# All products pass by pass, and new byte places for the operands of TensorE

## The chip, the cores and the metric

The kernel runs on one core of a Trainium2 chip. The metric is the device time of one execution in microseconds (us). Matrix products run on TensorE: the page calls its matmuls PE and its weight loads PEld. VectorE is DVE, ScalarE ACT, GpSimd POOL, SyncE SP. A matmul has a stationary operand, the weights (128 x 128, loaded before it), and a moving operand, here 128 partitions by 256 or 512 columns of 4 bytes, that streams past the weights.

## The reference

A trunk of two layers over 256 tokens with a model width of 1024, in float32. `swiglu` stands four times: before and after each layer's mixer.

```
x = x + 0.5 * swiglu(rmsnorm(x, norm_w[l, 0]), w_gate, w_up, w_down)     # d_ff = 2816
x = x + mixer(rmsnorm(x, norm_w[l, 1]))   # l = 0: Mamba-2 (SSD), l = 1: windowed attention over shared k, v
x = x + 0.5 * swiglu(rmsnorm(x, norm_w[l, 2]), ...)
swiglu(h) = (silu(h @ w_gate) * (h @ w_up)) @ w_down
```

k and v are computed once from the residual stream after layer 0. A final RMSNorm ends it.

## The kernel before

**Three products for one.** To keep float32 precision, each operand is split into a high part (rounded to the type float32r) and a low part (what the rounding left). A product is high x high + high x low + low x high: three matmuls per 128 x 128 block. Weights come from memory in chunks of 2 x 512 KB (`raw`); ACT writes the high part `hi` (L144), DVE the low part `lo` (L155), each a tile of 128 x 1024 in one pool of six buffers. A tile of weights is called a unit; `ORDER` lists the units, and `tick`, called after each, issues the rounding of later ones. SP issues the loads.

**First products.** The normed input lies in eight tiles `xs0` to `xs7`, each 128 x 512: the high part `xh` in the left 256 columns, the low part `xl` in the right 256. Units g and u (gate and up) go through `wide` (L354): a matmul of 512 columns does hi x xh and hi x xl at once, and one of 256 does lo x xh. Units dt, B, C, x, z (Mamba mixer) and qA, qB (attention) go through `unit` (L339), all with 256 columns. kA, kB and v use tiles of their own, `xkh` and `xkl`.

**Second products.** Units d (down), so (mixer out) and ao (attention out) go through `rows` (L372): for each of eight output blocks j, three matmuls of 256 columns with the moving operands `hh` and `hl` (also named `yh`, `yl`, `oh`, `ol`).

**Stages.** f0, the Mamba mixer, f1, f2, attention, f3. f0 to f3 are the four `swiglu`; each has 22 steps f of one g, one u and (from f = 4 on) one d unit, 16 + 16 + 24 = 56 matmuls, plus four d units behind. f2 also holds kA and kB (48 matmuls on L349).

**The order of the passes before.** The order on every engine is written out by hand. In `wide`, f1 and f2 (`l != i`) from f = 1 on run the eight 512-wide matmuls of `hi` and then the eight 256-wide of `lo` ("pass by pass"); f0 and f3 alternate, one of `hi`, one of `lo`. In `rows`, f1 and f2 run (hi,hh), (hi,hl), (lo,hh); all others (hi,hh), (lo,hh), (hi,hl). In `unit`, the x units and the very first unit run pass by pass, the others alternate.

**Places.** Tiles lie one behind another in the pools, so a tile's first byte falls at some place within a 512-byte block; a step of 128 columns of weights is 512 bytes, so all blocks of a weight tile, and all eight `xs` tiles, share a place. In the built program before: `hi` and `lo` at 160, `xs` at 480, `hh` and `hl` at 480, `xkh` and `xkl` at 160. The tile `ones`, which the warm-up uses for both operands, is at 128.

Of the kernel before, what the change touches and what calls it, by code (L numbers as in the profile page):

```python
# [9 lines left out]
F32 = mybir.dt.float32  # L10
F32R = mybir.dt.float32r
# [5 lines left out]
P = 128  # L17
T = 256
D = 1024
KT = D // P  # L20
# [13 lines left out]
CH = 2  # L34
RAW = 4
NEG = -1.0e30


def ffn_order(l, i):
# [36 lines left out]
ORDER = order()  # L76
# [33 lines left out]
class Weights:  # L110
# [38 lines left out]
    def low(self, half=None):  # L149
        u = self.cut  # L150
        c, i = divmod(u, CH)
        if not half:
            self.lo = self.parts.tile([P, D], F32R, tag="lo", name=f"lo{u}")
        hi, lo, s = self.ready.get(u, self.hi), self.lo, self.piece(half)
        self.nc.vector.tensor_tensor(lo[:, s], self.chunks[c][:, i, s], hi[:, s].bitcast(F32), ALU.subtract)  # L155
        if half == 0:
            return
        self.ready[u] = (hi, lo)
        self.cut += 1
        if i == CH - 1 or u == NU - 1:  # L160
            del self.chunks[c]
            self.load()
# [53 lines left out]
class Trunk:  # L216
    def __init__(self, ctx, tc, a):
# [2 lines left out]
        self.NPART = 6  # L220
        cp = self.cp = ctx.enter_context(tc.tile_pool(name="const", bufs=1))

        self.op = ctx.enter_context(tc.tile_pool(name="op", bufs=LAG + 2))
        top = ctx.enter_context(tc.tile_pool(name="top", bufs=1, side="right"))
        self.wk = ctx.enter_context(tc.tile_pool(name="work", bufs=2))
        raw = ctx.enter_context(tc.tile_pool(name="raw", bufs=RAW))
        parts = ctx.enter_context(tc.tile_pool(name="parts", bufs=self.NPART))
# [108 lines left out]
        nc.scalar.copy(rs, b[:, 0:256])  # L336
        return rs

    def unit(self, what, out, xh=None, xl=None, before=None):  # L339

        nc = self.nc
        xh = self.xh if xh is None else xh
        xl = self.xl if xl is None else xl
        hi, lo = self.W.next(what)
        passes = [(k, w, x) for k in range(KT) for w, x in ((hi, xh), (hi, xl), (lo, xh))]
        if self.W.pos == 1 or what[0] == "x":
            passes = [(k, w, x) for w, x in ((hi, xh), (lo, xh), (hi, xl)) for k in range(KT)]
        for n, (k, w, x) in enumerate(passes):
            nc.tensor.matmul(out, w[:, k * P : (k + 1) * P], x[k], start=n == 0, stop=n == len(passes) - 1)  # L349
        if before:  # L350
            before()
        self.tick()
# [16 lines left out]
        self.slots.run()  # L369
        self.W.ahead(self.NPART - 2)  # L370

    def rows(self, units, accs, first, last, done=None, high_first=False):  # L372

        nc = self.nc
        for j in range(KT):
            out = accs[j % 4][:, (j // 4) * T : (j // 4) * T + T]
            s = slice(j * P, (j + 1) * P)
            for n, ((hi, lo), hh, hl) in enumerate(units):
                f, e = first and n == 0, last and n == len(units) - 1
                passes = ((hi, hh), (hi, hl), (lo, hh)) if high_first else ((hi, hh), (lo, hh), (hi, hl))  # L380
                for m, (w, x) in enumerate(passes):
                    nc.tensor.matmul(  # L382
                        out, w[:, s], x, start=f and j < 4 and m == 0, stop=e and m == 2, skip_group_check=True
                    )
            if done:
                done(j, out)
# [90 lines left out]
    def ffn(self, l, i, key, nxt):  # L477
        nc, wk = self.nc, self.fw
# [24 lines left out]
        def product(name, f, t):  # L503

            b = self.bank(f"{name}_{key}_{f}")
            if self.W.pos == 0:
                self.slots.at(0, lambda: nc.scalar.copy(t, b[:, 0:T]))
                self.unit((name, l, i, f), b[:, 0:T])
                return

            def add():
                nc.scalar.copy(t, b[:, T:])  # L512
                nc.vector.tensor_tensor(t, b[:, 0:T], t, ALU.add)  # L513

            self.slots.at(0, add)
            self.wide((name, l, i, f), b, by_part=l != i and f > 0)

        for f in range(NF):
            g, u = (wk.tile([P, T], F32, tag=n, bufs=4, name=f"{n}s_{key}_{f}") for n in "gu")
# [14 lines left out]
    def down(self, l, i, f, hs, accs):  # L534
        hi_lo = self.W.next(("d", l, i, f))
        hh, hl = hs.pop(f)
        self.rows([(hi_lo, hh, hl)], accs, f == 0, False, high_first=l != i)
        self.tick()

    def tail(self, units, accs, nxt):  # L540
# [7 lines left out]
    def ssm(self, nxt):  # L548
# [9 lines left out]
        accs = []  # L558
# [264 lines left out]
        for what in seq[:-2]:  # L823
            if what[0] == "so":
                tt = what[1]
                if not accs:
                    accs = self.accs("sa")
                self.rows([(self.W.next(what), yh[tt], yl[tt])], accs, tt == 0, False)
                self.tick()
            else:  # L830
                o = half()
                self.unit(what, o, before=lambda: evac(what, o, E[what] - at[what]))
        self.tail([(w, yh[w[1]], yl[w[1]]) for w in seq[-2:]], accs, nxt)


# [29 lines left out]

    def split_k(self):
        wk = self.kp
        self.xkh = [wk.tile([P, T], F32R, name=f"xkh{k}") for k in range(KT)]
        self.xkl = [wk.tile([P, T], F32R, name=f"xkl{k}") for k in range(KT)]
        for k in range(KT):  # L870
# [34 lines left out]
    def att(self, nxt):  # L905
# [124 lines left out]
        for j in range(4):  # L1030
# [3 lines left out]
                sl.at(0, lambda: vdone(vb))  # L1034
                self.shared_v(1, vb)
            b = self.bank(f"q{j}")
            self.unit(("qA", j), b[:, 0:T])
            Q[j] = [wk.tile([P, T], F32, tag=f"Q{r}", name=f"Q{j}_{r}") for r in range(2)]

            def q_rope(j=j, b=b):  # L1040
# [194 lines left out]
```

## Time and profile before

| | before |
|---|---|
| median of 3 runs | 1048.29 us (1047.95 to 1049.29) |
| profiled execution | 1048.69 us |
| its span, first to last instruction | 1046.9 us |
| PE busy | 1025.2 us (98%), 7290 records |
| PEld busy | 948.2 us (91%) |
| DVE / ACT / POOL busy | 775.1 / 627.7 / 79.4 us |
| DMA | 190.84 MB, mean 182 GB/s |

The 1.8 us between the execution and its span lie before the first and behind the last instruction. Matmuls are pipelined: one that is busy for 278 ns overlaps the next, so the distance between the starts of two, not the duration, tells how fast they go. A timeline row of N matmuls runs from the start of the first to the end of the last; the chain's pieces follow each other without overlap, so a piece of N matmuls divided by N is their spacing. Some fp32 matmuls (warm-up, statistics) have two records each.

### The profile page before, as it was taken

Reading aid. Unit: us, or ns where it says so; the run is one execution under the profiler, and the core shown is the slowest. Engines: PE = TensorE matmul, PEld = TensorE weight load, DVE = VectorE, ACT = ScalarE, POOL = GpSimd, SP = SyncE. Lnnn points to the kernel's source line nnn. Section 1 sums busy time; section 2 is a strip of 40 time slices with the busy share of each in tenths; the row PEclk is TensorE's granted clock in tenths of the full one; section 3 lists DMA queues with packets and bytes.
Section 4 is the critical chain, followed back from the end, with each engine's and each line's share of the span. In section 5 each row is a group of like instructions: output and inputs, shape, how many; then the busy total and the mean of one; then the engine's idle time right before and its main releaser. Section 6 shows DMA issues by size and latency. Waiting matters only on the chain.

```text
span 1046.9 us, 18340 instructions
## 1 busy us (share of the span) xinstructions
PE 1025.2 (98%) x7290; PEld 948.2 (91%) x7290; DVE 775.1 (74%) x1420; ACT 627.7 (60%) x1106; POOL 79.4 (8%) x122
## 2 busy tenths in 40 slices
PE   8999999999999999999999999999999999999996
PEld 7899999999989898999999899999998888999996
DVE  4766666788999977766667796666689777666664
ACT  6555555669877756555555664555565766555554
POOL 3000000210110112000000200000031020000000
PEclk9999999999999999999999999999999999999998
DMA  8555554546545354555455455554554244555521
GB/s 304 195 201 176 186 200 164 194 171 252 217 156 213 131 201 153 197 201 200 169 203 200 157 211 200 177 209 178 202 202 152 92 161 167 196 186 191 187 101 40
DMA packets 30132, 190.84 MB, mean 182 GB/s; under 512 B 3904, under 2 KB 5728, under 8 KB 8544
## 3 DMA queue, kind: packets, MB, share of 16 engines
q1 hardware_dynamic: 30048, 189.69, 51.0%
q8 instruction: 57, 0.93, 0.4%
q14 instruction: 27, 0.22, 0.1%
HBM read 187.27 MB, written 1.10 MB: 180 GB/s over the span
## 4 chain that ended last, share of the span: by engine, by line
PE 80%; DVE 11%; ACT 3%; DMA 2%; POOL 1%; issue 1%; SPq 0%; ACTq 0%; DVEq 0%; POOLq 0%
PE u_f L362 23%; PE g_f L362 22%; PE da_f L382 22%; PE sa L382 3%; PE sb L349 3%; DVE lo L155 2%; DVE xs L394 2%; DMA csb<-cs_scratch 2%; PE aa L382 1%; PE q L349 1%; DVE xs L601 1%; DVE X L402 1%; DMA raw<-w 1%; DVE E L723 1%; ACT hi L144 1%
## 5 line engine op out<-in xcount | busy, mean ns | idle before, releaser
L155 DVE TENSOR_TENSOR lo<-raw,hi 128x1024 fp32r<-128x1024 f32 (+1 forms) x343 | 415.2, 1214 | 15.0 <-ACT hi L144 15.0
L144 ACT ACTIVATE hi<-raw 128x1024 fp32r<-128x1024 f32 (+1 forms) x343 | 357.3, 1047 | 18.9 <-PE da_f L382 5.1
L362 PE MATMUL u_f<-xs,hi 128*128 128x512 f32 x704 | 218.1, 397 | 0.0
L362 PE MATMUL g_f<-xs,hi 128*128 128x512 f32 x696 | 213.7, 395 | 0.8 <-DVE xs L394 0.8
L382 PE MATMUL da_f<-hh_f,hi 128*128 128x256 f32 x704 | 195.8, 278 | 0.0
L382 PE MATMUL da_f<-hh_f,lo 128*128 128x256 f32 x704 | 195.6, 278 | 0.0
L382 PE MATMUL da_f<-hl_f,hi 128*128 128x256 f32 x704 | 195.6, 278 | 0.0
L362 PEld LDWEIGHTS u_f<-xs,hi 128*128 128x128 f32 x704 | 130.1, 189 | 27.0
L362 PEld LDWEIGHTS g_f<-xs,hi 128*128 128x128 f32 x696 | 127.8, 188 | 27.2 <-DVE xs L394 2.2
L362 PE MATMUL u_f<-xs,lo 128*128 128x256 f32 x704 | 149.4, 280 | 0.0
L362 PE MATMUL g_f<-xs,lo 128*128 128x256 f32 x696 | 148.0, 281 | 0.0
L382 PEld LDWEIGHTS da_f<-hh_f,hi 128*128 128x128 f32 x704 | 132.3, 188 | 1.7
L382 PEld LDWEIGHTS da_f<-hl_f,hi 128*128 128x128 f32 x704 | 132.2, 188 | 0.0
L382 PEld LDWEIGHTS da_f<-hh_f,lo 128*128 128x128 f32 x704 | 132.1, 188 | 0.0
L513 DVE TENSOR_TENSOR gs_f<-g_f,gs_f 128x256 f32<-128x256 f32 x87 | 36.9, 424 | 113.7 <-ACT gs_f L512 113.6
L362 PEld LDWEIGHTS u_f<-xs,lo 128*128 128x128 f32 x704 | 114.1, 189 | 3.7
L362 PEld LDWEIGHTS g_f<-xs,lo 128*128 128x128 f32 x696 | 113.2, 188 | 3.3
L349 PE MATMUL sb<-xs,hi 128*128 128x256 f32 x656 | 108.0, 284 | 0.1
L513 DVE TENSOR_TENSOR us_f<-u_f,us_f 128x256 f32<-128x256 f32 x88 | 37.3, 424 | 88.8 <-ACT us_f L512 88.7
L512 ACT COPY us_f<-u_f 128x256 f32<-128x256 f32 x88 | 32.7, 371 | 111.4 <-PE u_f L362 111.3
L349 PEld LDWEIGHTS sb<-xs,hi 128*128 128x128 f32 x656 | 93.8, 190 | 1.2 <-issue 0.5
L512 ACT COPY gs_f<-g_f 128x256 f32<-128x256 f32 x87 | 32.1, 369 | 89.8 <-PE g_f L362 89.8
(252 smaller groups left out, 1369.4 us busy)
## 6 DMA issues: line engine op xcount, KB each, us to landing
raw<-w SPq DMA_DIRECT2D x168, 1024.0 KB, 4.9
csb<-cs_scratch SPq DMA_DIRECT2D x8, 768.0 KB, 7.0
raw<-w SPq DMA_DIRECT2D x4, 512.0 KB, 8.2
X<-x SPq DMA_DIRECT2D x4, 256.0 KB, 5.9
Q<-r_q SPq DMA_DIRECT2D x32, 32.0 KB, 1.9
out<-o SPq DMA_DIRECT2D x3, 256.0 KB, 2.2
ca<-const_att SPq DMA_DIRECT2D x1, 704.0 KB, 8.2
raw<-w SPq DMA_DIRECT2D x2, 256.0 KB, 5.2
```

What stands on the lines that cost most here:

```text
L144: self.nc.scalar.activation(hi[:, s], self.chunks[c][:, i, s], AF.Copy)
L155: self.nc.vector.tensor_tensor(lo[:, s], self.chunks[c][:, i, s], hi[:, s].bitcast(F32), ALU.subtract)
L349: nc.tensor.matmul(out, w[:, k * P : (k + 1) * P], x[k], start=n == 0, stop=n == len(passes) - 1)
L362: self.nc.tensor.matmul(out[:, 0:c], w[:, k * P : (k + 1) * P], x[k], start=n == 0, stop=n == len(passes) - 1, skip_group_check=True,)
L382: nc.tensor.matmul(out, w[:, s], x, start=f and j < 4 and m == 0, stop=e and m == 2, skip_group_check=True)
L394: nc.vector.scalar_tensor_tensor(self.xl[j], self.X[j], wcol(j), self.xh[j].bitcast(F32), ALU.mult, ALU.subtract)
L402: nc.vector.scalar_tensor_tensor(self.X[j], out, scale, self.X[j], ALU.mult, ALU.add)
L512: nc.scalar.copy(t, b[:, T:])
L513: nc.vector.tensor_tensor(t, b[:, 0:T], t, ALU.add)
L601: V.scalar_tensor_tensor(out, u[:, tap : tap + T], self.s("convw", tap * 24 + c), out, ALU.mult, ALU.add)
L723: V.tensor_tensor(f, f, c, ALU.mult)
```

## The change

It does four things. (1) `wide` runs pass by pass from f = 1 on in all four stages. (2) `rows` runs (hi,hh), (hi,hl), (lo,hh) everywhere. (3) `unit` runs pass by pass, hi x xh, hi x xl, lo x xh; the very first unit keeps hi x xh, lo x xh, hi x xl, and dt and the first qA (`fresh`) go on alternating. (4) Pads of 8, 72 and 80 float32 columns move tiles, and the `lo` tile of units g, u, dt, B, C, x, z, qA, qB is taken from column 48 of a tile 128 columns wider. Built, the places in a 512-byte block are: `hi` 192, `xs` 192, `lo` 384 for these units and 192 for all others, `hh` and `hl` 0, `xkh` and `xkl` 0.

```
+ROOM = 128
+PADS = (8, 72, 80)
+BEGIN = {w: 48 for w in ("g", "u", "dt", "B", "C", "x", "z", "qA", "qB")}
...
         if not half:
-            self.lo = self.parts.tile([P, D], F32R, tag="lo", name=f"lo{u}")
+            b = BEGIN.get(ORDER[u][0], 0)
+            self.lo = self.parts.tile([P, D + ROOM], F32R, tag="lo", name=f"lo{u}")[:, b : b + D]
...
+        pads = [ctx.enter_context(tc.tile_pool(name=f"pad{i}", bufs=1, side=s)) for i, s in enumerate(("left", "right"))]
+        for pool, n in zip(pads, PADS):
+            pool.tile([P, n], F32, name="pad")
...
-    def unit(self, what, out, xh=None, xl=None, before=None):
+    def unit(self, what, out, xh=None, xl=None, before=None, fresh=False):
...
-        passes = [(k, w, x) for k in range(KT) for w, x in ((hi, xh), (hi, xl), (lo, xh))]
-        if self.W.pos == 1 or what[0] == "x":
-            passes = [(k, w, x) for w, x in ((hi, xh), (lo, xh), (hi, xl)) for k in range(KT)]
+        first = self.W.pos == 1
+        parts = ((hi, xh), (lo, xh), (hi, xl)) if first else ((hi, xh), (hi, xl), (lo, xh))
+        passes = [(k, w, x) for w, x in parts for k in range(KT)]
+        if fresh:
+            passes = [(k, w, x) for k in range(KT) for w, x in parts]
...
-                passes = ((hi, hh), (hi, hl), (lo, hh)) if high_first else ((hi, hh), (lo, hh), (hi, hl))
+                passes = ((hi, hh), (hi, hl), (lo, hh))
...
-            self.wide((name, l, i, f), b, by_part=l != i and f > 0)
+            self.wide((name, l, i, f), b, by_part=f > 0)
...
     def split_k(self):
         wk = self.kp
+        wk.tile([P, PADS[2]], F32, name="pad")
```

The rest of the diff hands `fresh` through and drops the argument `high_first`. DVE, ACT, POOL and SP have the same instructions in the same order as before. On PE the order moves inside units; two places follow.

PE in f3, the g unit of step 5, before (a row: line, operation, output<-moving operand,weights, output size):

```order
L362 MATMUL g_f3_5_10268<-xs0_84,hi286_10145 128x512
L362 MATMUL g_f3_5_10268<-xs0_84,lo286_10172 128x256
L362 MATMUL g_f3_5_10268<-xs1_85,hi286_10145 128x512
L362 MATMUL g_f3_5_10268<-xs1_85,lo286_10172 128x256
L362 MATMUL g_f3_5_10268<-xs2_86,hi286_10145 128x512
```

The same place now:

```order
L372 MATMUL g_f3_5_10277<-xs4_96,hi286_10154 128x512
L372 MATMUL g_f3_5_10277<-xs5_97,hi286_10154 128x512
L372 MATMUL g_f3_5_10277<-xs6_98,hi286_10154 128x512
L372 MATMUL g_f3_5_10277<-xs7_99,hi286_10154 128x512
L372 MATMUL g_f3_5_10277<-xs0_92,lo286_10181 128x256
L372 MATMUL g_f3_5_10277<-xs1_93,lo286_10181 128x256
```

All eight matmuls of `hi` now stand ahead of the eight of `lo`, as in f1 and f2 before.

PE in f3, the d unit behind it, output blocks 0 and 1, before:

```order
L382 MATMUL da_f30_9923<-hh_f3_1_10048,hi288_10203 128x256
L382 MATMUL da_f30_9923<-hh_f3_1_10048,lo288_10230 128x256
L382 MATMUL da_f30_9923<-hl_f3_1_10049,hi288_10203 128x256
L382 MATMUL da_f31_9924<-hh_f3_1_10048,hi288_10203 128x256
L382 MATMUL da_f31_9924<-hh_f3_1_10048,lo288_10230 128x256
```

The same place now:

```order
L392 MATMUL da_f30_9932<-hh_f3_1_10057,hi288_10212 128x256
L392 MATMUL da_f30_9932<-hl_f3_1_10058,hi288_10212 128x256
L392 MATMUL da_f30_9932<-hh_f3_1_10057,lo288_10239 128x256
L392 MATMUL da_f31_9933<-hh_f3_1_10057,hi288_10212 128x256
L392 MATMUL da_f31_9933<-hl_f3_1_10058,hi288_10212 128x256
```

The matmul of the low weights has moved behind both of the high weights.

## Rows read from the trace of the kernel before

**Rows 1.** The page, parts 1 and 2: engines and granted clock (tenths).

```profile
PE 1025.2 (98%) x7290; PEld 948.2 (91%) x7290; DVE 775.1 (74%) x1420; ACT 627.7 (60%) x1106; POOL 79.4 (8%) x122
...
PEclk9999999999999999999999999999999999999998
```

**Rows 2.** Waits of PE: who for whom, us in total, times, longest.

```profile
PE st_yg L334 <- DVE dg_yg L329: 3.4, 3, 1.8
PE st_yg L309 <- POOL ss_yq L299: 1.2, 1, 1.2
...
PE s L919 <- DVE m L934: 0.2, 1, 0.2
```

**Rows 3.** Windows of ten steps in f1, f2, f0, f3: length, engines busy.

```profile
core 0: us, PE busy (x) PEld busy (x) DVE busy (x) ACT busy (x) POOL busy (x), PEclk, DMA share, GB/s
455.46:537.79 82.33, 82.33 (x563) 75.76 (x561) 55.90 (x91) 44.45 (x71) 0.00 (x0) 1.00 0.54 192
652.79:735.13 82.34, 82.34 (x563) 75.77 (x562) 55.91 (x91) 44.46 (x71) 0.00 (x0) 1.00 0.55 192
80.11:164.94 84.83, 84.83 (x563) 77.56 (x561) 55.90 (x92) 44.44 (x70) 0.00 (x0) 1.00 0.53 186
905.13:989.96 84.83, 84.83 (x563) 77.56 (x561) 55.90 (x91) 44.44 (x70) 0.00 (x0) 1.00 0.52 186
```

**Rows 4.** Timeline of PE in f1: start us, us, line, operation, count.

```profile
504.86 1.99 PE L362 MATMUL g_f<-xs,hi 128*128 128x512 f32 x8
506.68 1.11 PE L362 MATMUL g_f<-xs,lo 128*128 128x256 f32 x8
507.63 2.00 PE L362 MATMUL u_f<-xs,hi 128*128 128x512 f32 x8
509.46 1.07 PE L362 MATMUL u_f<-xs,lo 128*128 128x256 f32 x8
510.37 0.28 PE L382 MATMUL da_f<-hh_f,hi 128*128 128x256 f32 x1
```

**Rows 5.** Chain of work in f3, one step: start us, us, what.

```profile
905.29 2.83 PE g_f L362 x16
908.12 2.82 PE u_f L362 x16
910.94 2.83 PE da_f L382 x24
```

**Rows 6.** Chain of work: d in f0, mixer units, d in f1, kab in f2.

```profile
187.72 9.91 PE da_f L382 x84
...
212.06 5.66 PE sb L349 x48
...
568.16 9.53 PE da_f L382 x84
...
619.65 5.76 PE kab L349 x48
```

**Rows 7.** Timeline of PE in the mixer, an x unit.

```profile
217.88 1.21 PE L349 MATMUL sb<-xs,hi 128*128 128x256 f32 x8
218.93 1.10 PE L349 MATMUL sb<-xs,lo 128*128 128x256 f32 x8
219.87 1.34 PE L349 MATMUL sb<-xs,hi 128*128 128x256 f32 x10
```

**Rows 8.** Timeline of PE: warm-up at the high clock, transposes in attention.

```profile
6.06 1.39 PE L1066 MATMUL warm<-ones 128*128 128x128 f32 x11
...
808.25 1.03 PE L1000 MATMUL t<-co,S 128*128 128x128 f32 x8
```

**Rows 9.** Chain of work in the mixer: the transfers of csb, transposes.

```profile
236.56 9.20 DMA csb<-cs_scratch
...
331.01 7.66 DMA csb<-cs_scratch
...
352.60 0.44 PE xt L685 x4
```

**Rows 10.** Windows of the mixer: columns as in rows 3.

```profile
205.90:236.00 30.10, 30.10 (x250) 29.49 (x250) 24.34 (x49) 17.29 (x30) 5.78 (x13) 1.00 0.50 177
236.00:353.00 117.00, 113.09 (x944) 108.84 (x943) 107.97 (x213) 97.13 (x176) 14.19 (x21) 0.99 0.54 199
353.00:398.00 45.00, 44.36 (x379) 43.15 (x378) 36.66 (x64) 27.29 (x47) 7.00 (x10) 1.00 0.56 198
```

More of the change, by code (lines that the diff above doesn't have):

```diff
@@ L370, in tick, with rows @@
         self.W.ahead(self.NPART - 2)
-    def rows(self, units, accs, first, last, done=None, high_first=False):
+    def rows(self, units, accs, first, last, done=None):
         nc = self.nc
@@ L536, in down @@
         hh, hl = hs.pop(f)
-        self.rows([(hi_lo, hh, hl)], accs, f == 0, False, high_first=l != i)
+        self.rows([(hi_lo, hh, hl)], accs, f == 0, False)
         self.tick()
@@ L831, in ssm @@
                 o = half()
-                self.unit(what, o, before=lambda: evac(what, o, E[what] - at[what]))
+                self.unit(what, o, before=lambda: evac(what, o, E[what] - at[what]), fresh=what == ("dt",))
         self.tail([(w, yh[w[1]], yl[w[1]]) for w in seq[-2:]], accs, nxt)
@@ L1036, in att @@
             b = self.bank(f"q{j}")
-            self.unit(("qA", j), b[:, 0:T])
+            self.unit(("qA", j), b[:, 0:T], fresh=j == 0)
             Q[j] = [wk.tile([P, T], F32, tag=f"Q{r}", name=f"Q{j}_{r}") for r in range(2)]
```

## The prediction

> **What bounds the kernel now.** I read the page's first two parts, then who PE waits for, then the stages. PE is busy 98% of the span and its clock is granted at full level nearly throughout [rows 1]; its waits, 13 rows in all, sum to 11.6 us, the longest of them 3.4 us [rows 2]. So the time is set by how far apart PE starts its matmuls, and a matmul's mean duration (278 ns) says little, since it overlaps the next. Spacing has to be taken from start times.
>
> The trace already holds both orders. Ten steps (one step: a g unit, a u unit, a d unit; 56 matmuls) take 82.33 us in f1 and 82.34 in f2, but 84.83 us in f0 and in f3, with DVE and ACT doing the same work [rows 3]: 8.233 against 8.483 us a step. DVE is busy 55.90 us of these ten steps and DMA 0.54 of its share, so neither is the bound there. f1 and f2 run g and u pass by pass and d in the order high-high, high-low, low-high; f0 and f3 alternate.
>
> The spacings, by width of the moving operand, from differences of starts: in f1 the 512-wide high pass of g takes 6.68 − 4.86 = 1.82 us for 8, about 228.7 ns each; its low pass 0.95 us, 118 ns each; u's low pass 0.91 us, 113.4 ns each [rows 4]. In f3 a pair of one 512-wide and one 256-wide takes 353.4 ns (2.827 us over 8 pairs) and a d unit 2.83/24 = 118 ns [rows 5]. At 2.4 GHz 256 columns are 106.7 ns and 512 are 213.3. So every matmul costs more than its columns: by 6.7 ns (113.4), by 11 (118), or by 15 (228.7). This excess, some 7,000 times over, is what the change can touch.
>
> **Part 1, the order in f0 and f3.** DVE, ACT, POOL and SP keep their order; only PE's moves. g and u from f = 1 on become what f1 and f2 have, and d takes their order of passes. The price is read, not estimated: 8.483 − 8.233 = 0.250 us a step, 0.141 of it in g and u (2 × 2.827 against 2.774 + 2.739), the rest in d. 21 steps in each of two stages: 42 × 0.25 = 10.5 us, less nearly nothing for the first steps of f0, which wait. Nothing new is waited for: the low weights are needed later than before, the high ones no sooner than in f1.
>
> **Part 2, the order of the 256-wide units** (B, C, x, z, q). Costed at nothing: in the self mixer the x units already ran pass by pass and the others alternated, and 48 matmuls in a row of both kinds take 5.66 us, 118 ns each, while an x unit's low pass alone takes 0.94 us for 8, 118 as well [rows 6, 7]. dt and the first q unit keep their order, since their operands arrive one by one.
>
> **Part 3, the places.** Before, every product but k and v streams its moving operand from byte 480 of a 512-byte block against weights at 160, 320 bytes apart. Afterwards high weights and normed input both lie at 192 (0 apart), the low weights of first products at 384 and the d operands at 0 (320 apart). Two rows tell something of "0 apart". kab has weights and operands at 160: 48 matmuls in 5.76 us, 120.0 ns [rows 6], slower than 113.4 or 118. The warm-up has both at 128: starts 111 ns apart at the high clock (1.39 us for 11, less the last one's 0.28, over 10), each for 256 column steps [rows 8]. So the distance alone does not decide. What separates them is that 128 is a multiple of 64 and 160 is not. The excesses point the same way: 113.4 is 17 times 6.67 ns, 120.0 is 18 times, and 106.7 is 16 times, where 6.67 ns is 16 columns at 2.4 GHz, or 64 bytes of the operand. A 1,024-byte row that starts at 480 touches 17 pieces of 64 bytes, one that starts at 192 or 0 touches 16. All three new places (0, 192, 384) are multiples of 64, and the old ones (160, 480) are not. My reading, an inference from few rows, is that one piece, 6.67 ns, goes from each matmul.
>
> Bounds for the 512-wide matmul: 216 ns below (213.3 and some 2.5 ns more, since the transposes, which stream 128 columns only and load 128, come no closer than 107 to 110 ns, say 109 [rows 8, 9], 2.5 above 106.7), 240 above (kab's 120 twice). I take 228.7 − 6.7 = 222, nearest to the row of the same shape. For the 256-wide: 109 below, 120 above; I take 118 − 6.7 = 111, which also is the warm-up's spacing, and above the transposes' 109, where with half the columns the loads alone must set the pace (PEld is busy 75.76 of 82.33 us [rows 3], so loads are close behind).
>
> Step: 16 × 222.3 + 40 × 111 = 7,997 ns. f1 and f2: 8.233 − 7.997 = 0.236, times 42, 9.9 us. f0 and f3, order and place together: 0.486 × 42 = 20.4 us (10.5 of it is part 1). The self mixer has 41 + 16 units of 24 matmuls of 256, 1,368 times 6.7 ns, 9.1 us; but from 236 to 353 us the chain of work runs through csb's DMA (9.20 and 7.66 us), DVE and ACT and hardly touches PE, with DVE busy 107.97 of 117.00 us [rows 9, 10]. A faster PE is hidden there, so I count the other 76 of 192 us: 3.5 us. Attention, k and v: 20 units of 24, 480 × 6.7 = 3.2, less some that already ran at 113: 2.5. Sum 36.3 us. Against it: work that PE has in hand while a norm's statistics pass through DVE and POOL shrinks by 3%, so the waits of [rows 2] grow; 3 us. Net 33 us.
>
> Here the Trainium skill speaks against part 3. The page "SBUF — State Buffer", in "Who interferes with whom", gives PE two independent read ports and says "PE and ACT never wait on anyone"; its box on cachelines has lines of 16 bytes, and all places, old and new, are multiples of 16. By that page part 3 is worth nothing and the sum is part 1's alone. The trace disagrees in so far as kab and d, equal in shape, clock and number of loads, run at 120.0 and 113.4 ns [rows 6].
>
> The profiled execution is 1048.69 us, span 1046.9; the median of the runs is 1048.29. 1048.3 − 33 = **1015 us**.
>
> **Rivals.** (a) The place costs back a piece where both streams start together, as kab against d suggests: the 512-wide stay at 228.7 and the high passes of the 256-wide units at 118, only low passes and second products gain. Step 16 × 229 + 40 × 111 = 8,104 ns: 0.129 × 42 + 0.379 × 42 = 21.3, mixer 1.9, attention 1.5, less 3: **1027**. For it: kab. Against: the warm-up.
>
> (b) The places do nothing, so part 3 does not do what it says: 1048.3 − 10.5 = **1038**. For it: rows of one shape and one place already run at 113.4 in f1 and 118.0 in f0 [rows 6], so spacing depends on what preceded, not on place alone. Against: kab at exactly 120.0, which no d unit shows.
>
> (c) The whole excess goes. 216 and 109: step 7,824 ns, 0.409 × 42 + 0.659 × 42 = 44.9 us, mixer 4.5, attention 3.4, less 4 for waits: **999**. For it: the transposes' 109. Against: matmuls with both streams at full rate never come closer than 111. The Trainium skill's page "TensorE: Matmul & The Clock Gate", in "Wait — 56ns, not 53.3ns?", gives N/2.4 + 2.5 ns for back-to-back matmuls, 215.8 ns for 512 columns. No 512-wide row here reaches it.
>
> (d) Slower: two streams that start at one place hinder each other for the whole length of the wide matmul. Then a 512-wide costs two of kab's, 240 ns, and the fast chain of 113 that follows u's high pass is no longer entered, so all 256-wide take 117.8. Step 8,552 ns: +0.319 × 42 + 0.069 × 42 + 784 × 2.2 ns (the high passes of 49 units) = +18 us, **1066**. The point from which it decides: with the 256-wide at 117.8 the mean of the old steps (8.358) is reached at 228 ns for the wide ones; with them at 113.4, only at 239. For it: kab; today's wide matmul is already at 228.7, so little is needed if the fast chains are lost. Against: the warm-up again, and the d operands keep 320.
>
> **How the numbers follow.** The forecast, 1005 to 1024 around 1015: 0.48. (a) 0.17, (b) 0.12, (c) 0.12, (d) 0.08, nothing gained or lost on balance 0.03. The range: 1001 to 1040 holds the forecast, (a), (b) and the upper half of (c), some 0.83; it leaves out (d), no change, and a gain beyond (c)'s middle. A measurement of this kernel tells 0.2%, 2 us, from no change. Faster by more: 0.48 + 0.17 + 0.12 + 0.12 = 0.89; within: 0.03; slower: 0.08.
>
> **What would show it.** In the changed profile ten steps should take the same in all four stages; 80.0 us is the forecast, 81.0 is (a), 82.3 is (b), 78.2 is (c), over 84 is (d). The high pass of g (8 matmuls of 512) should take 1.78 us instead of 1.82; if it stays while d falls from 2.72 to 2.66 us, it is (a). If f0 and f3 end with steps unlike f1 and f2, part 1 is wrong. The mixer between csb's first and second transfer should hardly shorten. The prediction fails if pieces of 64 bytes are not what the excess consists of, or if steps below 8.0 us run into the weights' path: DVE needs 5.6 us a step and the loads of PEld 7.6, so PEld is the nearer.

## The result and the profile after

| | before | after |
|---|---|---|
| median, 4 runs each side by side | 1048.79 us (1047.95 to 1050.14) | 1054.77 us (1054.13 to 1055.20) |
| after / before | | 1.0055 (1.0038 to 1.0073) |
| profiled execution, its span | 1048.69, 1046.9 us | 1054.40, 1052.6 us |

The changed kernel is 0.55% slower: the forecast of 1015 us, and its range, missed on the side of rival (d).

The page of after, its first part, answers to [rows 1]: PE's share is unchanged.

```profile
PE 1030.6 (98%) x7290; PEld 953.8 (91%) x7290; DVE 775.3 (74%) x1420; ACT 627.9 (60%) x1106; POOL 79.7 (8%) x122
```

Windows of ten steps in f1, f2, f0, f3 of after (length, then each engine's busy time), against [rows 3]:

```profile
core 0: us, PE busy (x) PEld busy (x) DVE busy (x) ACT busy (x) POOL busy (x), PEclk, DMA share, GB/s
456.04:540.24 84.20, 84.20 (x562) 77.17 (x561) 55.92 (x92) 44.52 (x70) 0.00 (x0) 1.00 0.53 188
657.13:741.34 84.21, 84.21 (x563) 77.18 (x562) 55.92 (x92) 44.52 (x70) 0.00 (x0) 1.00 0.54 186
79.23:163.43 84.20, 84.20 (x562) 77.16 (x561) 55.91 (x92) 44.51 (x70) 0.00 (x0) 1.00 0.53 188
912.05:996.25 84.20, 84.20 (x562) 77.16 (x561) 55.91 (x92) 44.52 (x70) 0.00 (x0) 1.00 0.54 188
```

A step is 8.420 us in all four stages. The stages have become alike, as forecast, but at a value between the two old ones: f0 and f3 gain 0.063 us a step on 8.483, f1 and f2 lose 0.187 on 8.233. The clock is 1.00 in all eight windows, DVE, ACT and DMA do the same.

Where in the step: the timeline of PE in f1 of after (start, us, line, operation, count), against [rows 4]:

```profile
506.56 2.01 PE L372 MATMUL g_f<-xs,hi 128*128 128x512 f32 x8
508.41 1.10 PE L372 MATMUL g_f<-xs,lo 128*128 128x256 f32 x8
509.35 2.02 PE L372 MATMUL u_f<-xs,hi 128*128 128x512 f32 x8
511.21 1.11 PE L372 MATMUL u_f<-xs,lo 128*128 128x256 f32 x8
512.16 0.28 PE L392 MATMUL da_f<-hh_f,hi 128*128 128x256 f32 x1
...
514.98 1.32 PE L372 MATMUL g_f<-xs,hi 128*128 128x512 f32 x5
```

From starts: g's high pass 1.85 us (231 ns a matmul, was 228.7), u's 1.86 (232), u's low pass 0.95 (118.4 from unrounded starts, where it was 113.4), the d unit 514.98 − 512.16 = 2.82 us, 24 times 117.8 where f1 had 113.4. So of the 0.187 us lost in a step of f1, 24 × 4.4 ns = 0.106 lie in d, 0.04 in u's low pass and the rest in the two wide passes.

The chain of work of after (start, us, what): the d units behind f0 and f1, and kab, against [rows 6].

```profile
186.03 9.91 PE da_f L392 x84
...
571.26 9.91 PE da_f L392 x84
...
623.56 5.65 PE kab L359 x48
```

d in f1 has gone from 9.53 to 9.91 us, the value of f0 before. kab, whose operands the change took from 0 to 320 bytes from their weights, is quicker, 117.8 ns for 120.0.

By stretches of the trace, in us: a stage counts from the start of its first g unit to the start of its last, and what lies between two stages from there to the next first g unit (e1 and b6 are experiments, below):

| | f0 | mixer | f1 | behind f1 | f2 | attention | f3 |
|---|---|---|---|---|---|---|---|
| before | 174.6 | 216.6 | 164.0 | 19.1 | 170.0 | 94.9 | 168.9 |
| e1, order alone | 168.8 | 216.1 | 164.0 | 19.1 | 170.0 | 95.2 | 164.3 |
| after | 172.7 | 217.9 | 167.3 | 19.7 | 172.9 | 96.0 | 167.4 |
| b6 | 167.8 | 215.9 | 163.2 | 19.1 | 169.3 | 95.5 | 163.5 |

From before to e1 10.9 us go in f0, f3 and the mixer, and 0.3 come back in attention. From e1 to after 16.4 come back, in every stretch.

### The profile page after: what moved, and what is told of

It reads as the page before. It is cut to its first block, busy times and chain, and to the rows that moved or that the text cites. A ratio compares the mean times of both kernels' runs of the same rounds, so it can differ in the third digit from the quotient of the medians.

```text
span 1052.6 us, 18344 instructions
## 1 busy us (share of the span) xinstructions
PE 1030.6 (98%) x7290; PEld 953.8 (91%) x7290; DVE 775.3 (74%) x1420; ACT 627.9 (60%) x1106; POOL 79.7 (8%) x122
## 4 chain that ended last, share of the span: by engine, by line
PE 80%; DVE 11%; ACT 3%; DMA 2%; POOL 1%; issue 1%; SPq 0%; DVEq 0%; POOLq 0%
PE u_f L372 23%; PE da_f L392 22%; PE g_f L372 22%; PE sa L392 4%; PE sb L359 2%; DVE lo L160 2%; DVE xs L404 2%; DMA csb<-cs_scratch 2%; PE aa L392 1%; PE q L359 1%; DVE xs L611 1%; DVE X L412 1%; ACT hi L148 1%; DVE E L733 1%; DMA raw<-w 1%
## 5 line engine op out<-in xcount | busy, mean ns | idle before, releaser
L372 PE MATMUL u_f<-xs,hi 128*128 128x512 f32 x704 | 182.1, 396 | 0.0
L372 PE MATMUL g_f<-xs,hi 128*128 128x512 f32 x696 | 177.8, 393 | 0.8 <-DVE xs L404 0.8
L372 PEld LDWEIGHTS u_f<-xs,hi 128*128 128x128 f32 x704 | 126.4, 188 | 24.0
L372 PEld LDWEIGHTS g_f<-xs,hi 128*128 128x128 f32 x696 | 124.8, 188 | 25.0 <-DVE xs L404 1.7
L372 PEld LDWEIGHTS u_f<-xs,lo 128*128 128x128 f32 x704 | 97.5, 188 | 7.2
L372 PE MATMUL u_f<-xs,lo 128*128 128x256 f32 x704 | 102.1, 281 | 0.0
L372 PEld LDWEIGHTS g_f<-xs,lo 128*128 128x128 f32 x696 | 95.5, 188 | 6.8
L372 PE MATMUL g_f<-xs,lo 128*128 128x256 f32 x696 | 99.3, 279 | 0.0
L359 PE MATMUL sb<-xs,hi 128*128 128x256 f32 x656 | 89.6, 289 | 0.1
L359 PEld LDWEIGHTS sb<-xs,hi 128*128 128x128 f32 x656 | 83.2, 194 | 1.2 <-issue 0.5
```

The lines of the kernel that those rows point to most:

```text
L372: self.nc.tensor.matmul(out[:, 0:c], w[:, k * P : (k + 1) * P], x[k], start=n == 0, stop=n == len(passes) - 1, skip_group_check=True,)
```

## The experiments

The theory at the start: the order is worth about what the prediction said, and a place matters by how far the moving operand lies from its weights within 512 bytes. Its rivals: that pieces of 64 bytes count, as the prediction had it; that places do nothing. "Distance" below is the moving operand's place less that of the weights. A third possibility came up on the way, that the spacing of a matmul depends on those before it.

### One half of the change at a time: e1, e2, e4

**e1_order_only** has the new order with the places of before (`hi`, `lo` 160, `xs`, `hh`, `hl` 480; the fourth pad is explained below and is empty here):

```
-ROOM = 128
-PADS = (8, 72, 80)
+ROOM = 0
+PADS = (0, 0, 0, 0)
-BEGIN = {w: 48 for w in ("g", "u", "dt", "B", "C", "x", "z", "qA", "qB")}
+BEGIN = {w: 0 for w in ("g", "u", "dt", "B", "C", "x", "z", "qA", "qB")}
```

> The new order of passes with the places of before (weights 160, every other operand 480, 320 bytes from them; the k operands 160). Three theories. Order: running pass by pass is what lost, places do nothing: then this is as slow as the changed kernel, 1054 us, and a step takes 8.42 us. Places: the order gives what f1 and f2 of before show, and the new places lost more than that: a step takes 8.233 us in all four stages and the time is 1048.8 - 10.5 = 1038 us. Pieces of 64 bytes (the prediction's): the same 1038 us for this kernel, since nothing lies at a multiple of 64.

Measured: 1039.19 us (1037.40 to 1040.69), 0.9925 of before (0.9908 to 0.9941). Repeated as the base of the later runs (**e1_again**): 1039.04, 0.9911 (0.9895 to 0.9927).

> e1_order_only once more, on the chip of h5 and h6: a step 8.233 us, 1037 to 1039 us.

**e2_places_only** has the new places with the order of before (`unit` is put back too, not shown):

```
-            self.wide((name, l, i, f), b, by_part=f > 0)
+            self.wide((name, l, i, f), b, by_part=l != i and f > 0)
...
-                passes = ((hi, hh), (hi, hl), (lo, hh))
+                passes = ((hi, hh), (hi, hl), (lo, hh)) if high_first else ((hi, hh), (lo, hh), (hi, hl))
```

> The new places with the order of passes of before (f0 and f3 alternate, f1 and f2 run pass by pass, units alternate). Order theory: 1048.8 us, as before. Places theory: f1 and f2 take 8.42 us a step as in the changed kernel, f0 and f3 at least 8.42 and probably more than the 8.483 of before, the units of the mixer up to 2 ns a matmul more; 1055 to 1065 us. Pieces of 64 bytes: faster than before, 1020 to 1035 us.

Measured: 1054.73 us (1052.56 to 1056.15), 1.0067 of before (1.0051 to 1.0083). A step takes 8.42 us in f1 and f2 as expected, but 8.44 to 8.45 in f0 and f3, less than the 8.483 of before, where probably more was expected.

**e4_wide_order_only** is e1 with `unit` put back (not shown) and `rows` in the order (hi,hh), (lo,hh), (hi,hl) everywhere. So `wide` has the new order, and d the order of f0 and f3 before, in f1 and f2 too:

```
-                passes = ((hi, hh), (hi, hl), (lo, hh))
+                passes = ((hi, hh), (lo, hh), (hi, hl))
```

> Places of before; of the order only g and u of f0 and f3 are changed to pass by pass, d keeps (hi,hh), (lo,hh), (hi,hl) everywhere, f1 and f2 included, and the 256-wide units keep their old order. History theory: d runs at 113.3 ns because of what it is entered from, whichever order its passes have, so a step is 8.233 us in all four stages and the time that of e1_order_only, 1038 us. If the order of d's passes is what makes it fast, d takes 117.8 ns in all stages, a step 8.34 us, 1046 us.

Measured: 1036.67 us beside a before of 1048.0, one execution. Its chain of work in f3, one step:

```profile
914.03 2.77 PE g_f L374 x16
916.80 2.74 PE u_f L374 x16
919.54 2.72 PE da_f L394 x24
```

Windows of ten steps in f1 and f3 of e1, columns as above:

```profile
457.75:540.09 82.34, 82.34 (x563) 75.76 (x561) 55.92 (x91) 44.43 (x71) 0.00 (x0) 1.00 0.54 190
...
906.35:988.68 82.33, 82.33 (x563) 75.75 (x561) 55.90 (x91) 44.43 (x71) 0.00 (x0) 1.00 0.55 192
```

The order gives f3 the step of f1, 8.233 us for 8.483; that is worth 8 to 9 us, and e4 (8.233 in all four stages) shows that it is the order in g and u alone. d runs at 113.3 ns in e4 although its passes stand as in f0 before, where it ran at 118.0 [rows 6]. The places cost 16 us on top of the new order (1039 to 1055) and 7 on top of the old one, where f0 and f3 had no chain at 113 to lose. So the two do not add: at the new places the order gains nothing that shows (1054.73 in e2, 1054.77 after).

### Pieces of 64 bytes: e3

**e3_all_320_at_64** keeps the new order and every distance at 320, but moves everything by 32 bytes, so that all places are multiples of 64 (weights 192, all others 0; the k operands, at a distance of 0 in e1, go to 320 as well):

```
-PADS = (8, 72, 80)
+PADS = (8, 120, 80, 0)
-BEGIN = {w: 48 for w in ("g", "u", "dt", "B", "C", "x", "z", "qA", "qB")}
+BEGIN = {w: 0 for w in ("g", "u", "dt", "B", "C", "x", "z", "qA", "qB")}
```

> The new order, every operand 320 bytes from its weights as before, but all places multiples of 64 (weights 192, all others 0): against e1_order_only only the shift by 32 bytes differs, and the k operands, 320 instead of 0 from their weights. Places theory, with the distance alone deciding: the time of e1_order_only within 1 us, 1038, a step 8.233 us. Pieces of 64 bytes: 6.7 ns less for each matmul, a step near 7.95 us, 1010 to 1015 us. Order theory: 1054 us.

Measured: 1037.46 us (1036.57 to 1038.73), 0.9904 (0.9890 to 0.9919). Ten steps in f1 of e3:

```profile
457.75:540.09 82.34, 82.34 (x562) 75.76 (x562) 55.93 (x91) 44.48 (x71) 0.00 (x0) 1.00 0.54 190
```

To the hundredth the window of e1. Every matmul of the stage begins at a multiple of 64 now, and none is shorter: 228.6, 118 and 113.3 ns in both. The 64-byte reading is wrong. What the two kernels share, the distance, is what is left of the place.

e3 is also the closest control for the changed kernel: the same order, the same places of `hi`, `hh`, `hl`, `xkh` and `xkl`, and 320 for all low passes. Only the high passes of first products go from a distance of 320 to 0 (`xs` from 0 to 192, with `lo` of the first products moved along), and the time from 1037.46 to 1054.77 us. The chain of work of e3, d units behind f1 and kab:

```profile
562.50 9.53 PE da_f L396 x84
...
613.97 5.44 PE kab L363 x48
```

Both take longer after, 9.91 and 5.65 us, with their own operands at the very same places. They have taken over the pace of u's low pass ahead of them, 113.4 ns in e3 and 118.4 after.

### The distance: s2 to s6, c2

Each has the new order, one distance for all first products and kab, and another for d. A fourth pad ahead of the work pool, which holds the weights, moves these against `hh` and `hl`:

```
+        mid = ctx.enter_context(tc.tile_pool(name="mid", bufs=1))
+        if PADS[3]:
+            mid.tile([P, PADS[3]], F32, name="pad")
         self.wk = ctx.enter_context(tc.tile_pool(name="work", bufs=2))
...
-PADS = (8, 72, 80)
+PADS = (96, 48, 32, 32)
```

The last line is that of s2 (first products 128, d 192); the others differ in the four numbers alone: s3 192 and 256, s4 256 and 384, s5 384 and 448, s6 448 and 64, c2 352 and 288.

> The new order; normed input and k operands 128 bytes from all their weights, second products' operands 192 bytes from theirs. If the distance decides: d takes 113.3 ns a matmul, 2.72 us a unit, since the 48 matmuls of v at a distance of 192 in the changed kernel settled there within five, even when they started at 118 to 120; the first products at 128 are unknown, between 109 and 120 for 256 columns, 216 and 240 for 512. If distance does not decide, d takes 118 ns (2.83 us) whenever it is entered at 118, and the 256-wide first products 118 as well.

> The new order; normed input and k operands 192 bytes from all their weights, second products' operands 256 from theirs. Distance theory: every chain of 256-wide at 192 settles at 113.3 ns whatever it is entered from, as d did in s2_x128_d192 and v in the changed kernel: the low passes of g and u 113.3 ns, and the units of the mixer and of attention 113.3 instead of 118. The 512-wide at 192 is open, 216 to 240. d at 256 is open, 109 to 120. History theory (what ran before alone sets the pace of a chain): 118 ns in most chains that follow a wait.

> The new order; normed input and k operands 256 bytes from their weights, second products' operands 384 from theirs. Distance theory: each distance has its own spacing, the same in f1, f2, f0 and f3 and in the mixer; 256 agrees between the units here and d in s3_x192_d256. History theory: chains at one distance differ with what ran before them. The time lies between 1030 and 1055 us by either.

> The new order; normed input and k operands 384 bytes from their weights, second products' operands 448 from theirs. Distance theory: the units at 384 take what d takes in s4_x256_d384. For the 512-wide the table so far reads 228.7 ns at 320, 231 to 234 at 0 and at 128; 384 may be lower or higher, 216 to 240.

> The new order; normed input and k operands 448 bytes from their weights, second products' operands 64 from theirs. Distance theory: the units at 448 take what d takes in s5_x384_d448, and distances on both sides of 0 (64 and 448) are about as slow as 0 itself, 118 to 120 ns. For the 512-wide at 448: 229 to 240.

> The new order at distances that are no multiples of 64: normed input and k operands 352 bytes from their weights, second products' operands 288. If the spacing repeats every 128 bytes of distance (113.3 or 117.8 at 64, 192, 320, 448; 119 to 120 at 0, 128, 256, 384), these lie half way and take something between, 113 to 120; if only whole blocks of 64 bytes count, 352 and 288 act as the multiple of 64 below or above them: 320 or 384, 256 or 320.

Measured, one execution each: s2 1044.86 (before 1047.40); s3 1056.89, s4 1056.02, s5 1047.66, s6 1050.60 (before 1050.40); c2 1055.92 (before 1048.00). Spacings, ns, from unrounded starts (512 wide: the mean of a pass of eight, the middle one of all such passes):

| distance | 512 wide, g / u | 256 wide | read in |
|---|---|---|---|
| 0 | 231.1 / 232.1 | 120.0 | after; kab before |
| 64 | | 117.8 | d of s6 |
| 128 | 233.4 / 232.1 | 118.8 | s2, kab |
| 192 | 234.3 / 232.7 | 113.3 (d of s2, kab of s3); 117.8 (mixer units of s3) | s2, s3 |
| 256 | 232.1 / 229.8 | 120.0 | s4, kab |
| 288, 352 | 233.2 / 233.0 (352) | 116.8 (288), 120.0 (352) | c2 |
| 320 | 228.5 / 229.3 | 113.3 or 117.8 | e1, e3 |
| 384 | 233.4 / 232.1 | 118.8 | d of s4, kab of s5 |
| 448 | 232.7 / 232.7 | 113.3 | kab of s6, d of s5 |

Chains of work, 84 matmuls of d and 48 of kab, at 256 and 192 (s3), then at 384 and 256 (s4):

```profile
573.31 10.08 PE da_f L396 x84
...
625.75 5.44 PE kab L363 x48
```

```profile
570.81 9.99 PE da_f L396 x84
623.24 5.76 PE kab L363 x48
```

One operation of one shape, kab, takes 5.44 us in s3 and 5.76 in s4. For the 256-wide the multiples of 64 fall in three groups: 0 and 256 (120.0), 128 and 384 (about 119), and the odd multiples (113.3 or 117.8). The last group holds 64 and 448 too, which s6 was expected to show about as slow as 0. Of the distances of c2, 288 (116.8) lies between its neighbours as expected, and 352 (120.0) does not. The 512-wide are lowest at 320, but this column holds for these sequences alone: e5, below, has 227.8 at 0, and c1 231 and 234 at 320. None of these kernels is under e1: in all of them the wide matmuls are slower than there. Within a chain the weights in use and those loaded for the next matmul share a place, so no run tells which of the two the distance counts from.

### Distance is not enough: c1, e5

**c1_hi320_lo192_d192** puts together what the table offers: the wide pass at 320, low passes and d at 192, where d of s2 ran at 113.3.

```
-PADS = (8, 72, 80)
+PADS = (0, 96, 80, 32)
-BEGIN = {w: 48 for w in ("g", "u", "dt", "B", "C", "x", "z", "qA", "qB")}
+BEGIN = {w: 32 for w in ("g", "u", "dt", "B", "C", "x", "z", "qA", "qB")}
```

> The new order with distances chosen from the runs so far: normed input 320 bytes from the high weights, 192 from the low weights of first products, second products' operands 192, k operands 320. Distance with history: the 512-wide stay at 228.7 ns, d at 113.3 as in s2_x128_d192, and the low pass of g, which runs at 118 at a distance of 320, settles at 113.3 after two or three matmuls, as in s3_x192_d256; a step takes 8.20 us instead of 8.233, and so and ao run nearer 113 than 118: 1033 to 1036 us, 2 to 5 us below e1_order_only. Distance alone, without history: the same d and low passes. If the place plays no part, 1038 us as e1_order_only.

Measured: 1051.30 us (1049.64 to 1053.20), 1.0028 (1.0017 to 1.0038), a step 8.427 us: slower, where the table summed to less than e1. The low passes and d run near 118 although at 192, and the wide ones come 225 to 238 ns apart although at 320.

**e5_hi0_lo320_d192** is the changed kernel with d's operands at 192 in place of 320:

```
-PADS = (8, 72, 80)
+PADS = (0, 48, 80, 32)
```

> The changed kernel but for d's operands, 192 instead of 320 bytes from their weights (all places 96 bytes further on). Theory: of the 0.187 us a step that the changed kernel loses against e1_order_only, 24 times 4.5 ns, 0.108 us, is d's fast chain, lost because the wide pass at a distance of 0 hands it over at another moment; the rest is the wide pass itself and u's low pass. At 192 d falls to 113.3 ns from any start: a step 8.31 us, 1045 us. If d's pace comes from the distance of the normed input, d stays at 117.8 and a step at 8.42, 1054 us.

Measured: 1045.21 us, one execution. Its chain of work in f3, two steps:

```profile
912.39 2.77 PE g_f L376 x16
915.15 2.80 PE u_f L376 x16
917.96 2.83 PE da_f L396 x24
920.78 2.80 PE g_f L376 x16
923.59 2.76 PE u_f L376 x16
926.35 2.73 PE da_f L396 x24
```

The time is as expected, the way there is not: the same d unit, at the same places, takes 2.83 us in one step and 2.73 in the next. So 113.3 and 117.8 are two paces that one and the same chain can have, and something ahead of it chooses. The wide passes alternate as well: at one distance of 0, g and u take 228 ns a matmul in one step and 232 in the next.

### What chooses the pace: h6, h5, b6, b0

Starts of e1 show a pattern. Differences between starts, ns, in a step of e1, and in one of after (g high, g low, u high, u low, first of d):

```
e1     226 229 232 226 229 232 225 230 | 120 117 118 118 117 118 118 118
       229 232 225 230 231 226 229 232 | 113 114 113 113 114 113 113 114 | 113 113 114
after  241 224 231 236 228 233 231 226 | 117 118 118 117 119 117 118 116
       235 234 236 224 231 235 229 233 | 123 118 116 121 118 117 119 115 | 117 118 118
```

In e1 the wide ones come as 226, 229, 232 in turn. The rule read from it: a chain that follows 232 runs at 113, one that follows 226 or 229 at 118; it keeps its pace; and a pass that is entered at 113 begins its turn at 226, at 118 with 229. With eight wide ones g hands over at 118 and u at 113, so d runs at 113. Then the number of wide matmuls should decide. **h6_wide6** makes only the first six of a high pass 512 wide, the last two as pairs of 256:

```
+            high, low = passes[0::2], passes[1::2]
+            pair = [(k, w, x[:, s : s + T], s, T) for k, w, x, _, _ in high[6:] for s in (0, T)]
+            passes = high[:6] + pair + low
```

> e1_order_only (places of before, new order), but in g and u from f = 1 on only six of the eight high matmuls are 512 wide; the last two are done as four of 256, ahead of the low pass. History theory: entered from a chain at 113.3 the wide ones come 226, 229, 232, 226, 229, 232 ns apart, so the sixth hands over after 232 ns and the chain behind it runs at 113.3, in g as in u, and d as well: a step is 12 x 229 + 48 x 113.3 = 8.19 us, though it has four matmuls more than the 8.233 us of e1_order_only; 1034 to 1035 us, some 3 to 4 below e1. If history has no part and g's chain is slow for another reason, g's 12 stay at 117.8: 8.24 us, no gain on e1.

Measured: 1048.85 us (1047.26 to 1049.72), 1.0002 of before (0.9993 to 1.0011). Its windows of ten steps in f1, f2, f0, f3:

```profile
455.16:539.16 84.00, 84.00 (x602) 79.08 (x601) 55.89 (x92) 44.45 (x70) 0.00 (x0) 1.00 0.54 188
655.48:737.34 81.86, 81.86 (x602) 76.93 (x601) 55.90 (x91) 44.45 (x71) 0.00 (x0) 1.00 0.56 193
80.34:164.61 84.27, 84.27 (x603) 79.09 (x601) 55.88 (x92) 44.44 (x70) 0.00 (x0) 1.00 0.53 188
907.32:991.59 84.27, 84.27 (x603) 79.10 (x602) 55.89 (x92) 44.44 (x70) 0.00 (x0) 1.00 0.54 188
```

The same instructions at the same places take 8.186 us a step in f2 and 8.427 in f3. The chain of work in f2, then in f3:

```profile
663.83 2.73 PE g_f L379 x18
666.56 2.73 PE u_f L379 x18
669.29 2.72 PE da_f L399 x24
...
915.91 2.80 PE g_f L379 x18
918.71 2.80 PE u_f L379 x18
921.51 2.83 PE da_f L399 x24
```

```
f2     226 229 232 226 229 231 | 114 113 113 114 | 113 113 114 113
f1     229 231 226 229 232 226 | 117 119 117 118 | 118 118 117 118
f3     233 236 229 232 226 229 | 120 118 117 118 | 118 117 119 117
```

(Six wide, four of the pairs, the first four of the low pass.) In f2 and f1 six are two full turns: the pass gives back the pace at which it was entered. In f3 it begins 233 236 and ends at 229, and 118 stays as well. From step 2 on all four stages ran at 118, and only f2 left it, behind kA and kB. The chain of work there:

```profile
619.68 2.80 PE u_f L379 x18
622.48 5.76 PE kab L363 x48
628.24 2.83 PE da_f L399 x24
631.07 2.75 PE g_f L379 x18
633.81 2.73 PE u_f L379 x18
636.55 2.72 PE da_f L399 x24
```

The 48 matmuls of kab, at a distance of 0, run at 120.0 ns whatever they are entered from (117.8 here, 113.4 before). The next high pass of g comes 235 231 232 226 229 232, hands over at 113, and the stage keeps that. So the forecast of 1034 to 1035 us was missed because the entry from 113, which it took for granted, was there in f2 alone, from kab on. **h5_wide5** (five wide, three pairs: `high[5:]` and `high[:5]`) should alternate as eight do:

> As h6, with five of eight 512 wide and three as pairs of 256. History theory: from a chain at 113.3 the fifth hands over after 229 ns, so g's chain runs at 117.8; from that one the fifth of u hands over after 232 ns, so u's chain and d run at 113.3: the mixture of e1_order_only, a step 10 x 229 + 14 x 117.8 + 38 x 113.3 = 8.245 us, 1039 us. If the number of wide matmuls had no effect on the pace behind them, h5 and h6 would have the same paces.

Measured: 1038.64 us, one execution; steps of 8.247 us in all four stages. g ends 226 229 and hands over at 118, u ends 229 232 and hands over at 113.3, d runs at 113.3.

Two last kernels try to set the pace and then keep it. In steps 1 and 2 g has seven wide and u eight; from step 3 on **b6_set_then_keep** has six in both, and **b0_set_then_keep** none (0 in place of the 6):

```
+            m = (7 if what[0] == "g" else 8) if what[3] < 3 else 6
+            pair = [(k, w, x[:, s : s + T], s, T) for k, w, x, _, _ in high[m:] for s in (0, T)]
+            passes = high[:m] + pair + low
```

> Places of before, new order; g and u: in steps 1 and 2 seven high matmuls of 512 in g and eight in u, from step 3 on six in both, the rest as pairs of 256 ahead of the low pass. Theory: seven leave 117.8 whatever they find, eight turn that into 113.3, six keep it: a step 8.19 us in all four stages, 18 steps a stage at 0.046 us less than e1_order_only, 1034 to 1036 us. If what a stage starts with is not set by these counts, some stages run at 8.43 us a step as in h6, and the time lies between 1039 and 1050 us.

> As b6, but from step 3 on no high matmul is 512 wide: all 16 of a unit are 256 wide, 72 matmuls a step instead of 56. Theory: with no wide pass there is nothing that could hand over, the fast pace of step 2 lasts to the end of the stage, a step is 72 x 113.3 = 8.16 us, 1032 to 1035 us. If some chance delay flips it in a stage, that stage runs at 72 x 117.8 = 8.48 us.

b6: **1034.88 us (1034.10 to 1035.60), 0.9873 of before (0.9851 to 0.9894)**, the shortest of the study and below both kernels. b0: 1058.33 (1057.40 to 1059.07), 1.0093 (1.0076 to 1.0109). Ten steps in f1 of b6, then the chain of work in f3 of b0:

```profile
456.31:538.18 81.87, 81.87 (x602) 76.94 (x601) 55.91 (x91) 44.49 (x71) 0.00 (x0) 1.00 0.56 191
```

```profile
914.61 2.83 PE g_f L380 x24
917.44 2.83 PE u_f L380 x24
920.26 2.83 PE da_f L400 x24
```

b0 missed its expectation and tells why: without wide matmuls all 72 of a step run at 2.83 / 24 = 117.8 ns to the end of each stage. The setting had not worked. In b6, too, starts of steps 1 and 2 show the chains behind seven and behind eight at 118 (but for u of step 1 in f0, which follows a wait); only g of step 3, with six, went 235 231 232 226 229 232 (in f1) and on to 113, and all four stages of b6 stay at 8.187 us a step. So that a chain keeps its pace, and that six wide keep a pace of 113 as well, is shown. That b6 came to 113 at all is luck: neither setting worked, and its time is as forecast by another way.

The rule had a pass that is entered at 118 begin at 229, and these begin at 233 or 235. A d unit ahead of them does not decide: in f3 of h6 the passes of steps 2 and 3, which have none, begin 233 236 like the later ones. The starts of the nine traces that have first products at 320 throughout (before, e1 twice, e3, e4, h5, h6, b6, b0) tell more. Every high pass whose last spacing was 226 or 229 led into 118, and all but one of 654 with 232 into 113. The last spacing (to the first 256-wide behind the pass) and the number of 256-wide matmuls go with how the next pass begins (within 2 ns; passes with a wait left out):

| last spacing | 256-wide until the next pass | the next pass begins | times |
|---|---|---|---|
| 232 | 8 to 38, at 113 | 226 229 232 | 602 |
| 229 | 8 or 14, at 118 | 229 232 226 | 437 |
| 229 | 12 or 36 | 233 236 229 | 86 |
| 226 | 8 or 14 | 235 232 232 | 19 |
| 226 | 10 | 233 236 229 | 6 |
| 226 | 12 or 36 | 229 232 226 | 40 |

Lengths that differ by a multiple of six act alike. This explains b6: seven wide that begin 235 and eight that begin 233 both end at 226; eight 256-wide later the next pass begins 235 again, and six of that end at 232. It was read after the runs, and no kernel was built to test it.

## Why the prediction was wrong

**Part 1, the order, held.** f0 and f3 took the step of f1, 0.250 us less. Predicted 10.5 us; e1's median is 8.2 us under before, e1_again's 9.4, and the profiled executions differ by 10.6 over the stretches. That d gains by its own order was not part of the sum, but "d takes their order of passes" suggests it: by e4 d's order does nothing, and d gains by what it is entered from.

**Part 2, at nothing, held.** The mixer shortened by 0.5 us in e1.

**Part 3 is the step that failed**, in size and in sign: −22 us in the sum, +16 measured (e1 to after). The inference "one piece, 6.67 ns, goes from each matmul" fell in e3, and rivals (a) and (c), which count in the same pieces, with it. What the new places did was to put the high passes at a distance of 0: the wide matmuls went from 229 to 231 and 232 ns, and the chains behind them from 113.3 to 117.8. The inference came from two mistakes. One was the row chosen: for "0 apart" there were kab at 120.0 [rows 6] and the warm-up at 111 [rows 8], and I took the warm-up, which is fp32, writes 128 columns and has two records for each matmul, over the row with the type and shape of the products. kab's price is what the 256-wide at 0 then had, 120.0. The other was to read 113.4, 118 and 120 as lengths of one matmul. 113.3 and 117.8 are two paces of the same chain at the same place, so no count of pieces in an operand can tell them apart. The trace before held that too: d in f0 and f1, same places, 118.0 and 113.4 [rows 6], and 118 is no whole number of pieces (17.7). I used that row for rival (b) and not against my own.

**Rival (d) came nearest.** "The fast chain of 113 that follows u's high pass is no longer entered" is what after shows: the 256-wide of f0 to f3 take 117.6 to 118.4 on average. Its reason for the wide, that two streams from one place hinder each other for the whole length, is not shown; e5 has wide passes at 228 at the same distance. Its term for the wide was too large, 240 ns against 231 to 232. With 231 in place of 240 its step is 16 × 231 + 40 × 117.8 = 8,408 ns, against 8,420 measured; with 1,344 wide matmuls (42 + 42 steps of 16) the 9 ns are 12 us, and its 1066 becomes 1054. That this is the measured time to 1 us is in part luck: its 2.2 ns for each high pass of a unit were not paid in the mixer, since the low passes ran at 113.4 behind high ones at 120.0, and 48 matmuls took 5.64 us as before. Its deciding point was right as well: with the 256-wide at 117.8, 228 ns for the wide, and 231 lies above. I gave it 0.08, since "the d operands keep 320" spoke against it. That was the error about history once more: d kept its place and lost its pace, because the wide pass ahead of it had another place.

**Rival (b), places do nothing,** gave 1038, which is e1's time. The Trainium skill's page "SBUF — State Buffer", section "Who interferes with whom", was weighed for it; by its rule the places would be worth nothing. Two kernels that differ in places alone, e1 and after, are 16 us apart, so here the measurement decides and the places matter, though no run shows that it is reading that collides. e3 against e1, a move of everything by 32 bytes with no effect, does agree with that page's box on lines of 16 bytes.

**What I said of the surroundings.** The stretch between csb's two transfers stayed, 94.5 us before and 94.1 after (starts 234.81 and 328.92). PE's waits stayed as they were, the largest sum 3.4 us for st_yg as in [rows 2] (three waits; the longest single one was 1.8 us and is 2.0); the 3 us that I set aside for them had no faster PE to come from. A step below 8.0 us, where loads were to set the pace, was reached by no kernel; b6's 8.187 is the shortest. Two slips in the working change nothing: 1.82 us over 8 is 227.5 ns, where 228.7 stands (unrounded starts give 228.6), and (c)'s terms sum to 7,816 ns, not 7,824. That the loads alone set the transposes' 109 ns was not tested.

## What to carry to other kernels

Where TensorE is busy throughout and the clock is full, take the spacing of starts for each shape, and when one operation at one place shows two spacings in one trace, ask what runs ahead of it before giving the place a price. Take the price of a new place from the row with the same type, shape and distance, here kab, and try order and place as separate kernels, each with the other old and new: here the order was worth −8 to −9 us at the old places and nothing at the new. A pace that a stage inherits from what ran long before, as in h6, can make small edits far away look good or bad, so compare the windows of all stages and not the total alone.

## What the runs showed of the hardware

- At full clock, with weights loaded for each matmul, the spacing of float32r matmuls changes with the distance of moving operand and weights within 512 bytes: at multiples of 64 bytes 256 columns settle at 113.3, 117.8, about 119 or 120.0 ns, and a pass of 512 takes 228 to 234 a matmul. Moving both by 32 bytes changes nothing (e1, e3). Why, no run shows.
- At distance 320 a chain of 256-wide matmuls has two paces, 113.3 and 117.8 ns, and keeps the one it began with through whole stages (b0: 72 a step at 117.8, to the end). A pass of 512-wide ones can change it: apart from at most their first three they come as 226, 229 and 232 ns in turn, and where the pass ends in that turn goes with the pace of what follows (e1, h5, h6). At a distance of 0 a chain settles at 120.0 from either pace (kab before and in h6).
- Six wide matmuls of eight, with the other two as pairs, cost less a step than eight (8.187 against 8.233 us) where the chain is at 113, and more (8.400 or 8.427) where it is at 118. Which pace a stage has goes back to the last wide passes and chains before it, by the table above, which no kernel was built to test; what the first pass behind a wait does remains open.
